# The first feed-forward's beginning: one written order for three engines, constant matmuls where the matrix engine waits, the norm weight loaded as rows, 1/rms by a square root

## Chip, cores and metric

The kernel runs on one core of a Trainium2 chip. The metric is the device time of one execution in microseconds (us); several executions are made and the median is given. The core has five engines with a queue of instructions each: TensorE (PE, matrix products; its weight loads are shown apart as PEld), VectorE (DVE), ScalarE (ACT), GpSimd (POOL) and SyncE (SP), which here only issues DMA transfers. An engine takes its queue strictly in order; an instruction whose operands aren't ready holds up all that stand behind it. PE writes to PSUM, eight banks of 128 x 512 floats; the other data lies in SBUF with 128 partitions.

## What is computed

One encoder layer over two independent sequences of 512 tokens with 1024 channels, in float32: a half-step SwiGLU feed-forward, a mixing block (attention and a matrix memory), a second half-step feed-forward, and a norm. The change touches only the beginning of the first feed-forward:

```python
def rms_norm(x, g):
    y = x * lax.rsqrt(jnp.mean(x * x, axis=-1, keepdims=True) + EPS)
    return y * g

def swiglu(x, w_gate, w_up, w_down):
    return (jax.nn.silu(x @ w_gate) * (x @ w_up)) @ w_down

x = x + 0.5 * swiglu(rms_norm(x, ffn1_norm), ffn1_w_gate, ffn1_w_up, ffn1_w_down)
```

`w_gate` and `w_up` are 1024 x 2816, 22 blocks of 128 columns.

## The kernel before

**Products.** Each float32 matrix is split into a high part, rounded to the format that PE multiplies in one pass (`fp32r`), and a low part, the rest; a product is high x high + high x low + low x high. So each 128 x 512 piece of x and each weight costs ACT one cast (high part) and DVE one subtraction (low part). Gate and up, and the two sequences (`x_prompt`, s = 0, and `x_sample`, s = 1), are combined as the two rows and two columns of a 2 x 2 product with seven multiplications; the seven right-hand operands are the tiles `xc[B11]`, `xc[B21]`, `xc[B22]`, `xc[T1]` to `xc[T4]`. Two of them, B11 and B21, are x_prompt's lower and upper four groups of 128 channels alone; the other five need sums with x_sample.

**The beginning** (from line 1229). x comes in four blocks of 128 tokens per sequence (`load_x`, tile `raw`). `rows_rstd` squares each block, the left half on DVE and the right half on ACT, sums them, and takes 1/rms by a bit trick with three Newton steps, twelve DVE instructions on 128 x 4 elements (`rstd_cols`, `rsqrt_cols`). `turn` transposes a group of 128 channels on PE with the tile `ident` into a PSUM bank, `keep_x` copies it to SBUF on ACT and stores it in `xbuf`. `bcast_psum` turns 1/rms into a 128 x 512 tile with four transposes. `first_x` scales a group (`scaled`: times the norm weight `g1`, times 1/rms; DVE) and splits it (`put`: high on ACT, low on DVE). While x_sample is being prepared, PE begins the products that need x_prompt alone: `up.begin(j, W)` makes for column block j the first product (12 matmuls, B11), parks it in DRAM (`kept`), and makes the second (B21, 12 more). Ten blocks, `AHEAD`, are begun so: 240 matmuls. Then `up.rest` runs the other products (PSUM tiles `pss` and `pst`) of all 22 blocks.

**What sets the order.** A scheduler places the instructions on each engine by priority, as the code is written; `shifted(n)` moves a piece in priority, `tc.keep_in_program_order` (`pin`) keeps an instruction at its written place among the pinned ones of its engine. Weights come by `fetch_w` into tiles `wr` (four buffers) and are split into tiles `w` (four). All loads and stores of this part are issued by SP in the order of its queue. PSUM tiles named `mm` have three banks, `pss` and `pst` two each, `pso` one. Eight matmuls on the tile `ones` (line 1231) stand at the very beginning of PE. `g1` is loaded by POOL, element by element (line 123), and so are the weights of later norms and gates (`mix_gains`, written behind step 13 of `up.rest` but put by POOL's queue at the program's start).

## Time and profile before

| | us |
|---|---|
| median of 3 runs | 2079.39 (2077.46 to 2080.35) |
| the profiled execution, its own time | 2079.39 |
| its span, first to last instruction | 2077.5 |
| PE busy / DVE busy / ACT busy | 2059.7 / 1547.5 / 901.6 |
| PE at the first product of x and a weight | 18.18 |
| first product behind the ten begun blocks (`pss`) | 79.17 |

In the profile a row of the timeline gives the start, the time from the first start to the last end of the instructions that it merges, the engine, the line, the operation, out <- in, the shape and the count; in brackets the idle time before it and who ended it. The time of one instruction contains its fill and drain, which overlap with the next: three in a row take less than three times one. In the table by stretches the columns are the stretch, its length, the busy time of PE, PEld, DVE, ACT and POOL with the number of instructions, then the clock that PE was granted (1 is full), the mean busy share of the DMA engines, and GB/s.

### The profile page before, as it was taken

The page shows a single profiled execution, that of the slowest core. Times are in us where ns is not written, and L with a number is a line of the kernel's source. Part 1 is how long each engine was busy: PE and PEld are TensorE (multiplying, and loading weights), DVE is VectorE, ACT ScalarE, POOL GpSimd, SP SyncE. Part 2 cuts the span into 40 slices and gives each one's busy share as a digit, 9 for nine tenths or more (in the row PEclk, how much of TensorE's full clock was granted, in tenths as well). Part 3 has the DMA queues.
Part 4 walks back from the last instruction along what each step waited for, and adds up shares of the span by engine and source line. Part 5 has one row for each costly group of instructions (what it writes and reads, how often), then busy time and mean ns, then how long its engine had stood idle before and what let it go on. Part 6 is the DMA issues. An engine that isn't in the chain of part 4 may idle for free.

```text
span 2077.5 us, 27122 instructions
## 1 busy us (share of the span) xinstructions
PE 2059.7 (99%) x9451; PEld 1689.1 (81%) x9451; DVE 1547.5 (74%) x2798; ACT 901.6 (43%) x1653; POOL 103.7 (5%) x118
## 2 busy tenths in 40 slices
PE   8999999999999999999999999999999999999998
PEld 6888888888888877888877788888888888888887
DVE  7888888786797897575567645545888888796697
ACT  6544444442234566463344443323544444443224
POOL 1000000001003000100120000002000000000001
PEclk9999999999999999999999999999999999999999
DMA  9656555699766654777675245677656555599753
GB/s 280 206 171 195 193 172 183 197 338 365 267 218 239 219 159 170 260 240 271 218 270 176 102 152 183 204 255 239 210 168 220 176 190 182 166 346 350 267 204 125
DMA packets 307064, 454.31 MB, mean 219 GB/s; under 512 B 20064, under 2 KB 178864, under 8 KB 305904
## 3 DMA queue, kind: packets, MB, share of 16 engines
q1 hardware_dynamic: 304912, 446.87, 64.0%
q0 software_dynamic: 1872, 5.46, 0.8%
q8 instruction: 74, 1.21, 0.2%
q14 instruction: 62, 0.51, 0.1%
q10 hardware_dynamic: 144, 0.26, 0.0%
HBM read 285.63 MB, written 166.89 MB: 218 GB/s over the span
## 4 chain that ended last, share of the span: by engine, by line
PE 94%; DVE 2%; DMA 1%; ACT 1%; issue 0%; SPq 0%; ACTq 0%; DVEq 0%
PE mm L770 20%; PE pss L333 17%; PE pst L333 11%; PE mm L333 10%; PE mm L589 8%; PE pst L589 4%; PE pss L589 4%; PE mm L754 4%; PE pso L589 3%; PE pso L1044 1%; PE pss L1017 1%; PE pso L754 1%; PE pst L1036 1%; PE pso L1180 1%; PE pst L770 1%; PE pss L770 1%
## 5 line engine op out<-in xcount | busy, mean ns | idle before, releaser
L770 PE MATMUL mm<-xh,w 128*128 128x512 f32 x896 | 290.4, 394 | 0.0
L333 PE MATMUL pss<-xc,w 128*128 128x512 f32 x1056 | 256.3, 391 | 0.4 <-DVE t L364 0.4
L333 PE MATMUL mm<-xc,w 128*128 128x512 f32 x1056 | 253.1, 390 | 2.0 <-ACT w L291 1.0
L333 PE MATMUL pst<-xc,w 128*128 128x512 f32 x1056 | 253.8, 389 | 0.0
L333 PEld LDWEIGHTS pss<-xc,w 128*128 128x128 f32 x1056 | 196.9, 188 | 47.6 <-DVE t L364 7.0
L333 PEld LDWEIGHTS mm<-xc,w 128*128 128x128 f32 x1056 | 197.4, 188 | 44.8 <-ACT w L291 1.9
L333 PEld LDWEIGHTS pst<-xc,w 128*128 128x128 f32 x1056 | 198.1, 188 | 41.5 <-ACT t L368 0.4
L770 PEld LDWEIGHTS mm<-xh,w 128*128 128x128 f32 x896 | 167.7, 188 | 33.6
L589 PE MATMUL mm<-rt,w 128*128 128x512 f32 x765 | 178.8, 389 | 0.0
L770 PE MATMUL mm<-xl,w 128*128 128x512 f32 x448 | 176.3, 394 | 0.0
L589 PEld LDWEIGHTS mm<-rt,w 128*128 128x128 f32 x765 | 143.5, 188 | 29.8
L291 ACT ACTIVATE w<-t 128x512 fp32r<-128x512 f32 x176 | 106.9, 627 | 139.0 <-issue 55.2
L292 DVE TENSOR_TENSOR w<-t,w 128x512 fp32r<-128x512 f32 x176 | 118.1, 688 | 55.7 <-ACT w L291 53.8
L333 PE MATMUL pss<-xc,f 128*128 128x512 f32 x528 | 126.8, 389 | 0.0
L333 PEld LDWEIGHTS pss<-xc,f 128*128 128x128 f32 x528 | 99.1, 188 | 20.6
L672 ACT ACTIVATE w<-wr 128x512 fp32r<-128x512 f32 x72 | 45.1, 632 | 138.5 <-PE pso L589 65.2
L672 ACT ACTIVATE w<-t 128x512 fp32r<-128x512 f32 x82 | 51.8, 632 | 107.4 <-PE pst L589 62.4
L770 PEld LDWEIGHTS mm<-xl,w 128*128 128x128 f32 x448 | 84.3, 188 | 16.6
L589 PE MATMUL pss<-rt,w 128*128 128x512 f32 x396 | 93.7, 389 | 0.0
L589 PE MATMUL pst<-rt,w 128*128 128x512 f32 x396 | 93.7, 389 | 0.0
L239 ACT ACTIVATE w<-wr 128x1024 fp32r<-128x1024 f32 (+1 forms) x56 | 57.2, 1027 | 74.0 <-PE mm L770 30.3
L589 PEld LDWEIGHTS pst<-rt,w 128*128 128x128 f32 x396 | 74.3, 188 | 15.4
(359 smaller groups left out, 3653.6 us busy)
## 6 DMA issues: line engine op xcount, KB each, us to landing
rt<-rbuf SPq DMA_DIRECT2D x154, 512.0 KB, 5.5
wpark<-w SPq DMA_DIRECT2D x104, 512.0 KB, 3.4
w<-wpark SPq DMA_DIRECT2D x104, 512.0 KB, 4.6
wr<-in_ffn_w_gate_dram SPq DMA_DIRECT2D x62, 512.0 KB, 5.3
rbuf<-tab SPq DMA_DIRECT2D x102, 256.0 KB, 4.0
wr<-in_ffn_w_up_dram SPq DMA_DIRECT2D x44, 512.0 KB, 4.6
rbuf<-f SPq DMA_DIRECT2D x72, 256.0 KB, 4.0
wr<-in_w_in_dram SPq DMA_DIRECT2D x36, 512.0 KB, 6.0
```

The lines of the kernel that those rows point to most:

```text
L239: pin(nc.scalar.activation(hi, raw, AF.Copy))
L291: pin(nc.scalar.activation(t[:, 0], src, AF.Copy))
L292: pin(V_.tensor_tensor(t[:, 1], src, f(t[:, 0]), op=ALU.subtract))
L333: nc.tensor.matmul(p, a[:, k, :], xt[:, b, k, :], start=(first and k == 0 and i == 0), stop=(k == HK_ - 1 and i == 2), skip_group_check=True)
L589: nc.tensor.matmul(p, u[:, a, d * P:(d + 1) * P], r[:, b, ts], start=(first and q == 0 and k == 0), stop=(q == len(us) - 1 and k == 2), sk ...
L672: nc.scalar.activation(hi, src, AF.Copy)
L754: nc.tensor.matmul(p[b][:, :N], a[:, k, bs], w_[:, kl, :], start=(k == 0 and i == 0), stop=(k == KD - 1 and i == 2))
L770: nc.tensor.matmul(p, a[:, k, :], b, start=(k == 0 and i == 0), stop=(k == n - 1 and i == 2))
L1017: nc.tensor.matmul(p, qT[:, h, b * P:(b + 1) * P], kv[:, hk * 2 + j, :], start=(j == 0), stop=(j == 1))
L1036: nc.tensor.transpose(p[:, b * P:(b + 1) * P], Ps[b][:, kb * P:(kb + 1) * P], ident)
L1044: nc.tensor.matmul(po, Vst[:, kv_, hk, :], w, start=(kv_ == 0 and i == 0), stop=(kv_ == 3 and i == 1))
L1180: nc.tensor.matmul(po, vm[:, a, t, hs_], b, start=(t == 0 and n == 0), stop=(t == 3 and n == 2))
```

## The change

1. `g1` is no longer loaded element by element by POOL but as eight rows of 128, issued by ACT, and transposed by one small PE transpose.
2. `mix_gains` gets a tile of step 13 (`h[0]`) and copies from it first, so that POOL's loads can only run then.
3. The eight matmuls on `ones` are replaced by constant matmuls 128 x 512 on a tile `hot` (`busy(n)`): six at the start, two behind each of the first three blocks of x, three behind the last and three behind the broadcast of 1/rms, 18 in all. Their result isn't used.
4. x_prompt is transposed block by block as it arrives, into seven banks at once, instead of group by group.
5. 1/rms is ACT's square root and DVE's reciprocal in place of the twelve DVE steps. The dummy activation at the start now loads the table with the root, and a second one behind the root of x_sample loads the table with Silu.
6. The beginning is written as a list of steps that pins ACT's and DVE's order (`eps`, for the roots, is now set at the program's start): copies, scalings, high and low parts, weights in halves of four channel groups, squares of x_sample, parked products. Blocks 0 and 1 run both of their products in it; the third waits until x_sample's 1/rms is there.
7. SP's order: the first weight in two halves right behind x_prompt; the up-weight of block 0 is fetched later, and the weight of block 3 earlier.

**PE, the program's start.** Before the change (`pst_93` is the bank of the constant matmuls, `raw_267` x_prompt, `rs_352` 1/rms):

```order
L1231 MATMUL pst_93<-ones 128x128 x8
L1251 MATMUL mm_354<-ident,raw_267 128x128 x4
L1251 MATMUL pss_361<-ident,raw_267 128x128 x4
L1251 MATMUL pst_368<-ident,raw_267 128x128 x4
L1251 MATMUL mm_375<-ident,raw_267 128x128 x4
L1251 MATMUL pss_382<-ident,raw_267 128x128 x4
L1251 MATMUL pst_389<-ident,raw_267 128x128 x2
L213 MATMUL pst_413<-ident,rs_352 128x128 x4
```

In the change, PE from the last block of x_prompt to the first products (`mm_94<-xc_316` are the constant matmuls, `raw_260` x_prompt, `cs_38_336` 1/rms, `w_406` and `w_407` the weights of column blocks 0 and 1):

```order
L1253 MATMUL mm_334<-ident,raw_260 128x128
L1235 MATMUL mm_94<-xc_316 128x512 x3
L1321 MATMUL pst_389<-ident,cs_38_336 128x128 x4
L1253 MATMUL pst_394<-ident,raw_260 128x128 x4
L1235 MATMUL mm_94<-xc_316 128x512 x3
L333 MATMUL mm_435<-xc_316,w_406 128x512 x7
L333 MATMUL mm_448<-xc_316,w_407 128x512 x2
L333 MATMUL mm_435<-xc_316,w_406 128x512 x3
L333 MATMUL mm_448<-xc_316,w_407 128x512 x3
```

The broadcast of 1/rms stood behind six groups and now stands behind all blocks of seven groups, which by then are transposed but for the last block; constant matmuls stand on both sides of it.

**ACT, behind x_prompt.** Before, from the last high part of x_prompt (`R_285<-raw_268` with `cs` are squares of x_sample, L341 and L348 the first and second product of a block):

```order
L278 ACTIVATE xc_419<-t_18_281 128x512
L1270 ACTIVATE R_285,cs_55_523<-raw_268 128x512
L1270 ACTIVATE tab_286,cs_56_524<-raw_268 128x512
L1256 ACTIVATE R_285<-pss_568 128x512
L348 ACTIVATE f_19_282<-mm_432 128x512
L672 ACTIVATE f_9_272<-wr_555 128x512
L341 ACTIVATE f_20_283<-mm_494 128x512
```

In the change, from the same place (L1369 parks a first product, L1342 squares x_sample, L1395 is its root, L1377 is `gate`, the second product):

```order
L1346 ACTIVATE xc_317<-t_18_274 128x512
L1369 ACTIVATE f_20_276<-mm_448 128x512
L1342 ACTIVATE xc_318,cs_41_402<-raw_261 128x1024
L1353 ACTIVATE w_408<-wr_313 128x512 x2
L1257 ACTIVATE R_278<-pss_496 128x512
L1257 ACTIVATE tab_279<-pst_501 128x512
L1395 ACTIVATE cs_42_403<-cs_41_402,eps 128x4
L1396 ACT_TABLE_LOAD
L1396 ACTIVATE warm<-ones 128x1
L291 ACTIVATE w_565<-wr_563 128x1024
L291 ACTIVATE w_629<-wr_627 128x1024
L1377 ACTIVATE f_19_275<-mm_435 128x512
```

The second product of block 0, `mm_435`, is now taken out of its bank behind the squares, the root, a table load and the weights 3 and 4; a second square of x_sample that stands between the two casts and the two copies is left out of these rows.

**POOL, the program's start.** Before (`gain`, `gbias` and `hn` are `mix_gains`' tiles):

```order
L123 DMA g_84<-in_ffn_norm_dram 128x8x1
masks.py:197 MEMSET ident 128x128
L229 COPY wr_311<-raw_267 128x1
L691 DMA gain_96<-in_mix_norm_dram 128x8x1
L691 DMA gain_97<-in_ffn_norm_dram 128x8x1
L692 DMA gbias<-in_mlstm_gate_bias_dram 128x16
L693 DMA hn<-in_mlstm_head_norm_dram 128x4x1
```

In the change (`t_15_271` is `h[0]` of step 13):

```order
masks.py:197 MEMSET ident 128x128
L690 COPY gain_97<-t_15_271 128x8
L692 DMA gain_97<-in_mix_norm_dram 128x8x1
L692 DMA gain_98<-in_ffn_norm_dram 128x8x1
L693 DMA gbias<-in_mlstm_gate_bias_dram 128x16
L694 DMA hn<-in_mlstm_head_norm_dram 128x4x1
```

`g1` is gone from POOL's queue, and the other four loads stand behind a copy that waits for step 13. From the transposes of x_sample's last groups on, the order of PE, DVE and ACT is the same in both programs.

```diff
@@ -120,16 +120,16 @@
         return ap.bitcast(F32)
 
     g1 = cpool.tile([P, KD], F32, name="g1")
-    nc.gpsimd.dma_start(g1, I["ffn1_norm"][0].rearrange("(k p) -> p k", p=P))
-
+    eps = cpool.tile([P, 1], F32, name="eps")
+    nc.vector.memset(eps, EPS)
 
     ident = cpool.tile([P, P], F32, name="ident")
     make_identity(nc, ident)
     ones = cpool.tile([P, P], F32, name="ones")
     nc.vector.memset(ones, 1.0)
-    pw = PT()[:, 0:P]
+    pw = MM()
     warm = cpool.tile([P, 1], F32, name="warm")
-    nc.scalar.activation(warm, ones[:, 0:1], AF.Silu)
+    nc.scalar.activation(warm, ones[:, 0:1], AF.Sqrt)
...
                 if i == at:
-                    hook()
+                    hook(h[0])
...
-    def mix_gains():
+    def mix_gains(behind):
         pin = tc.keep_in_program_order
+        pin(nc.gpsimd.tensor_copy(gm, behind[:, 0:KD]))
         for t, n in ((gm, "mix_norm"), (g2, "ffn2_norm")):
             pin(nc.gpsimd.dma_start(t, I[n][0].rearrange("(k p) -> p k", p=P)))
...
-    for _ in range(8):
-        pin(nc.tensor.matmul(pw, ones, ones, start=True, stop=True))
+
+    def busy(n):
+
+        for _ in range(n):
+            pin(nc.tensor.matmul(pw, hot[:, 0:P], hot, start=True, stop=True))
+
...
...
+    def load_x(s, b):
+        nc.sync.dma_start(raws[s][:, b, :], xins[s][b * P:(b + 1) * P, :])
+
+    def turn(s, k, b, p):
+        return nc.tensor.transpose(p[:, b * P:(b + 1) * P], raws[s][:, b, k * P:(k + 1) * P], ident)
+
+    def keep_x(s, k, p, xt, eng=None):
+
+        i = eng.tensor_copy(xt, p) if eng else nc.scalar.activation(xt, p, AF.Copy)
         nc.sync.dma_start(xbuf[s][:, k, :], xt)
+        return i
 
     orow = up.ring.rows["o"]
 
-    def rows_rstd(s, engines):
-
...
+    def squares(s, b, sq, engines, pin=lambda i: i):
+        for i in range(2):
+            x_, to = raws[s][:, b, i * S:(i + 1) * S], sq[i][:, b:b + 1]
+            if engines[i] is V_:
+                pin(V_.scalar_tensor_tensor(orow[3 + i], x_, 1.0, x_, op0=ALU.mult, op1=ALU.mult, accum_out=to))
+            else:
+                pin(nc.scalar.activation(orow[3 + i], x_, AF.Square, accum_out=to))
+
+    def square_cols():
+        return [spool.tile([P, 4], F32, tag="cs4", bufs=4, name=nm("cs4")) for _ in range(2)]
+
+    def rows_rstd(sq, between=None):
+        pin(V_.tensor_tensor(sq[0], sq[0], sq[1], op=ALU.add))
+        pin(nc.scalar.activation(sq[1], sq[0], AF.Sqrt, scale=1.0 / D, bias=eps))
+        if between:
+            between()
+        pin(V_.reciprocal(sq[1], sq[1]))
+        return sq[1]
 
     def scaled(to, x_, k, R_):
-        V_.scalar_tensor_tensor(to, x_, g1[:, k:k + 1], R_, op0=ALU.mult, op1=ALU.mult)
-
-    load_x(0)
-    raw0 = up.fetch(0, (0,), raws[0][:, 1, 0:1])
-    load_x(1)
-    raw1 = [up.fetch(j, (0,))[0] for j in (1, 2)]
+        return V_.scalar_tensor_tensor(to, x_, g1[:, k:k + 1], R_, op0=ALU.mult, op1=ALU.mult)
+
     x0 = up.ring.rows["x"]
     x0r = orow[:2] + up.ring.rows["s"] + orow[5:7] + orow[2:3]
...
+    for b in range(4):
+        load_x(0, b)
+    raw0 = [wpool.tile([P, KD, P], F32, tag="wr", bufs=4, name=nm("wr"))]
+    for a in range(2):
+        nc.sync.dma_start(half(raw0[0], a), half(up.v[0], a)[:, :, 0:P])
+    load_x(1, 0)
+    raw1 = up.fetch(1, (0,))
+    for b in range(1, 4):
+        load_x(1, b)
+    raw1 += up.fetch(2, (0,))
+    g1row = orow[6][0:KD, 0:P]
+    pin(nc.scalar.dma_start(g1row, I["ffn1_norm"][0].rearrange("(k p) -> k p", p=P)))
+    raws0 = raw0 + raw1
+    for i in (B11, B21, T2_):
+        xc[i] = xc_tile()
+    hot = xc[B11][:, 0, 0, :]
+    nc.vector.memset(f(hot), 1.0)
+    busy(6)
+    banks = [PT(), PT()]
+    pin(nc.tensor.transpose(banks[1][:, 0:KD], g1row, ident[0:KD, 0:KD]))
+    pin(V_.tensor_copy(g1, banks[1][:, 0:KD]))
+    banks += [b() for b in (PS, PS, PO, MM, MM)]
+    sq = square_cols()
+    for b in range(4):
+        for k, p in enumerate(banks):
+            pin(turn(0, k, b, p))
+        squares(0, b, sq, (V_, nc.scalar), pin)
+        if b < 3:
+            busy(2)
+    pin(keep_x(0, 0, banks[0], x0r[0]))
+    rs = rows_rstd(sq, lambda: pin(keep_x(0, 1, banks[1], x0r[1], V_)))
+    busy(3)
+    R0 = PT()
+    for b in range(4):
+        pin(nc.tensor.transpose(R0[:, b * P:(b + 1) * P], rs[:, b:b + 1].to_broadcast([P, P]), ident))
+    banks.append(PT())
+    for b in range(4):
+        pin(turn(0, KD - 1, b, banks[-1]))
+    busy(3)
+
+    def keep(k, eng=None):
+        pin(keep_x(0, k, banks[k], x0r[k], eng))
+
+    def lo(k):
+        t = xc[B11 if k < HK_ else B21]
+        pin(V_.tensor_tensor(t[:, 1, k % HK_, :], x0[k], f(t[:, 0, k % HK_, :]), op=ALU.subtract))
+
+    sq = square_cols()
+
+    def square1(b, eng=None):
+        x_, to = raws[1][:, b, :], sq[0][:, b:b + 1]
+        junk = xc[T2_].rearrange("p a k c -> p (a k c)")
+        if eng:
+            pin(V_.scalar_tensor_tensor(junk[:, 2 * S:4 * S], x_, 1.0, x_, op0=ALU.mult, op1=ALU.mult, accum_out=to))
+        else:
+            pin(nc.scalar.activation(junk[:, 0:2 * S], x_, AF.Square, accum_out=to))
+
+    W = [w8_tile() for _ in range(2)]
+    def hi(k):
+        pin(nc.scalar.activation(xc[B11 if k < HK_ else B21][:, 0, k % HK_, :], x0[k], AF.Copy))
+
+    def sc(k):
+        pin(scaled(x0[k], x0r[k], k, R0))
+
+    def wh(j, a):
+        w = wt[j][:, :, a]
+        pin(nc.scalar.activation(w[:, 0], half(raws0[j], a), AF.Copy))
+
+    def wl(j, a):
+        w = wt[j][:, :, a]
+        pin(V_.tensor_tensor(w[:, 1], half(raws0[j], a), f(w[:, 0]), op=ALU.subtract))
+
+    wt = [w8_tile() for _ in range(3)]
+    W = [{B11: part(w, 0), B21: part(w, 1)} for w in wt]
+    X = [None] * 3
+
+    def first(j):
+        X[j] = MM()
+        product(X[j], W[j][B11], xc[B11], True)
+
+    def park(j):
+        up.kept[j], t = kept[j], up.ring("k")
+        pin(nc.scalar.activation(t, X[j], AF.Copy))
+        nc.sync.dma_start(kept[j][0], t)
+
+    def second(j):
+        product(X[j], W[j][B21], xc[B21], False)
+
+    def gate(j):
+        t = up.ring("k")
+        pin(nc.scalar.activation(t, X[j], AF.Silu))
+        nc.sync.dma_start(kept[j][1], t)
+
+    p1 = {}
+
+    def turn1(k):
+        for kk, bank in ((k, PS), (k + HK_, PT)):
+            p1[kk] = bank()
+            for b in range(4):
+                (turn if k else lambda *a: pin(turn(*a)))(1, kk, b, p1[kk])
+
+    def keep1(k):
+        for kk, kr in ((k, orow[3]), (k + HK_, orow[4])):
+            (keep_x if k else lambda *a: pin(keep_x(*a)))(1, kk, p1[kk], kr)
+
+    with shifted(-400):
+        for step in (wh, 0, 0), (keep, 2), (keep, 3), (sc, 0), (hi, 0), (wl, 0, 0), (keep, 4), (sc, 1), (hi, 1), (lo, 0),                 (wh, 1, 0), (sc, 2), (hi, 2), (lo, 1), (keep, 5), (sc, 3), (hi, 3), (lo, 2), (wl, 1, 0), (square1, 0),                 (wh, 0, 1), (lo, 3), (first, 0), (first, 1), (sc, 4), (hi, 4), (wl, 0, 1), (keep, 6), (sc, 5), (lo, 4),                 (hi, 5), (park, 0), (keep, 7), (sc, 6), (lo, 5), (hi, 6), (wh, 1, 1), (sc, 7), (lo, 6), (hi, 7), (wl, 1, 1), (lo, 7),                 (park, 1), (second, 0), (turn1, 0), (second, 1), (square1, 1), (wh, 2, 0), (wh, 2, 1), (wl, 2, 0), (wl, 2, 1), (square1, 2),                 (keep1, 0), (square1, 3, V_):
+            step[0](*step[1:])
+        pin(nc.scalar.activation(sq[1], sq[0], AF.Sqrt, scale=1.0 / D, bias=eps))
+        pin(nc.scalar.activation(warm, ones[:, 0:1], AF.Silu))
+        pin(V_.reciprocal(sq[1], sq[1]))
+    gate(0)
+    gate(1)
     up.begin(2, W[2])
-    rs = rows_rstd(1, (nc.scalar, nc.scalar))
-    raw0 += up.fetch(0, (1,))
     R1 = orow[2]
-    V_.tensor_copy(R1, bcast_psum(rs))
-    for i in (T2_, T1, T3, B22, T4):
+    with shifted(-100):
+        V_.tensor_copy(R1, bcast_psum(sq[1]))
+    for i in (T1, T3, B22, T4):
         xc[i] = xc_tile()
     x1 = up.ring.rows["s"] + [orow[5]]
     for k in range(HK_):
         x1l, x1u = x1[2 * k % 4], x1[(2 * k + 1) % 4]
-        for t, kk, bank, kr in ((x1l, k, PS, orow[3]), (x1u, k + HK_, PT, orow[4])):
-            p = turn(1, kk, bank)
-            keep_x(1, kk, p, kr)
-            scaled(t, p, kk, R1)
+        if k:
+            turn1(k)
+            keep1(k)
+        scaled(x1l, p1[k], k, R1)
+        scaled(x1u, p1[k + HK_], k + HK_, R1)
         for j in ((3,), (4, 5), (6, 7), (8, 9))[k]:
-            up.begin(j, up.left(j))
+            with shifted(-100):
+                w = up.left(j)
+            up.begin(j, w)
+        if k == 2:
+            raw0 = up.fetch(ORDER[0])
         put(xc[B22], k, x1u)
         right_sums(xc, k, x0[k], x0[k + HK_], x1l, x1u)
     up.begun()
```

40 lines of the change are left out of this document (removed).

## The prediction

> **What bounds the kernel now.** I read the page first: the share of busy time, then the chain of waits.
>
> ```profile
> span 2077.5 us, 27122 instructions
> PE 2059.7 (99%) x9451; PEld 1689.1 (81%) x9451; DVE 1547.5 (74%) x2798; ACT 901.6 (43%) x1653; POOL 103.7 (5%) x118
> PE 94%; DVE 2%; DMA 1%; ACT 1%; issue 0%; SPq 0%; ACTq 0%; DVEq 0%
> ```
>
> TensorE (PE) is busy 99% of the span and carries 94% of the chain: whatever else the change does, it can gain only the 17.8 us in which PE idles, or PE work that it takes away. It takes none of the products away. Next the table by stretches of time, to see where those 17.8 us lie.
>
> ```profile
> 4.60:8.00 3.40, 0.52 (x3) 0.14 (x1) 1.13 (x4) 1.18 (x4) 2.27 (x4) 0.97 0.95 227
> 11.40:14.80 3.40, 3.31 (x17) 2.91 (x16) 1.56 (x10) 2.88 (x8) 0.24 (x1) 0.52 1.16 244
> 14.80:18.20 3.40, 2.28 (x20) 1.80 (x18) 3.00 (x4) 3.40 (x7) 0.00 (x0) 1.00 1.03 380
> 100.00:400.00 300.00, 300.00 (x1316) 246.20 (x1316) 250.79 (x390) 130.97 (x218) 0.00 (x0) 1.00 0.56 182
> ```
>
> From 100 us on PE does not stop; the change must earn its gain in the first 80 us. The rows also show the granted clock (third number from the end): behind a stretch with PE busy 0.52 of 3.40 us stands one at half clock, and behind a full one the full clock. Last the timeline of PE, then VectorE (DVE) and ScalarE (ACT), over that beginning.
>
> ```profile
> 18.18 0.50 PE L333 MATMUL mm<-xc,w 128*128 128x512 f32 x1 [0.54 <-ACT xc L278]
> 22.71 11.21 PE L333 MATMUL mm<-xc,w 128*128 128x512 f32 x48 [0.27 <-DVE w L292]
> 33.76 0.60 PE L213 MATMUL pst<-ident,rs 128*128 128x128 f32 x4
> 36.48 4.86 PE L333 MATMUL mm<-xc,w 128*128 128x512 f32 x20 [0.77 <-ACT w L291]
> 65.47 13.86 PE L333 MATMUL mm<-xc,w 128*128 128x512 f32 x60
> 79.17 2.88 PE L333 MATMUL pss<-xc,w 128*128 128x512 f32 x12
> 85.18 3.04 PE L333 MATMUL pss<-xc,w 128*128 128x512 f32 x12 [0.41 <-DVE t L364]
> ```
>
> The first product starts at 18.18 and PE runs without a gap only from 22.71; one more wait, 0.77 us, is for the fourth weight. 240 matmuls (ten blocks of columns, 24 each) stand before the `pss` products at 79.17. One costs 0.228 us (60 in 13.7); a group of four transposes 0.44 us (0.60 less the overlap), 0.11 each. From the transposes at 65 us to 79.17, and on to the wait at 85.18, the order of every engine is the same in both programs, so 79.17 is my finishing post: what PE gains up to there is the gain of the whole.
>
> **The chain ahead of the first product.**
>
> ```profile
> 4.33 0.69 DVE L1268 SCALAR_TENSOR_TENSOR R<-raw 128x512 f32<-128x512 f32 x1 [3.32 <-DMA raw<-in_x_prompt_dram]
> 5.77 0.69 DVE L1268 SCALAR_TENSOR_TENSOR R<-raw 128x512 f32<-128x512 f32 x1 [0.74 <-DMA raw<-in_x_prompt_dram]
> 8.49 0.69 DVE L1268 SCALAR_TENSOR_TENSOR R<-raw 128x512 f32<-128x512 f32 x1 [2.02 <-DMA raw<-in_x_prompt_dram]
> 9.92 0.69 DVE L1268 SCALAR_TENSOR_TENSOR R<-raw 128x512 f32<-128x512 f32 x1 [0.73 <-DMA raw<-in_x_prompt_dram]
> g<-in_ffn_norm_dram POOLq DMA_DIRECT2D x1, 4.0 KB, 7.4
> 5.85 0.93 POOL L691 DMA_DIRECT2D gain<-in_mix_norm_dram  x1
> ```
>
> The four blocks of x arrive 1.44, 2.72 and 1.43 us apart. The long gap is where the gain `g1` is under way: 4 KB, element by element, issued by POOL, 7.4 us to land. The change loads it as eight rows and moves POOL's four other small loads (the first issued at 5.85) out of the beginning, so I let the third gap fall to the others: 9.92 - 1.28 = 8.64. In the rest of the stretch the DMA moved 380 GB/s (14.80:18.20), at which 512 KB takes 1.38 us: 4.33 + 3 x 1.38 = 8.5. I take 8.3, allowing that the second gap had a share of the same disturbance; the bounds are 8.3 and 9.92. The eight rows of `g1` are now ahead of the transposes in PE's order. A load like it isn't in the trace: at best it is there with x, at worst it takes 7.4 us again and is there at about 9.5, inside the bound 9.92. Nearest is the first block of x, in use at 4.33; the rows are issued one table load later (1.28, a row below), so 5.6, and PE then makes up two blocks (14 transposes and 4 fillers, 2.5 us) by 8.1. I take nothing for it.
>
> ```profile
> 9.91 0.63 ACT L1270 ACTIVATE tab<-raw 128x512 f32<-128x512 f32 x1 [0.71 <-DMA raw<-in_x_prompt_dram]
> 10.54 0.58 ACT L1256 ACTIVATE f<-mm 128x512 f32<-128x512 f32 x1
> 10.72 0.16 DVE L1271 TENSOR_TENSOR cs<-cs,cs 128x4 f32<-128x4 f32 x1
> 13.11 0.16 DVE L192 SCALAR_TENSOR_TENSOR rs<-rs,rs 128x4 f32<-128x4 f32 x1
> 15.20 1.41 DVE L1275 SCALAR_TENSOR_TENSOR t<-f,g,pst 128x512 f32<-128x512 f32 x2 [1.93 <-ACT t L1256]
> 25.75 2.09 DVE L279 TENSOR_TENSOR xc<-t,xc 128x512 fp32r<-128x512 f32 x3
> 2054.91 0.30 ACT L1433 ACTIVATE fs<-cs,eps 128x4 f32<-128x4 f32 x1 [5.39 <-DVE cs L205]
> ```
>
> Before, 5.28 us pass from the last block (9.92) to the first scaled row (15.20): squares and their sum until 10.88, twelve small DVE steps until 13.27, then PE is still in transposes at half clock. After: sum at +0.96; ACT, having copied one bank, takes the root (0.30, the row at 2054.91 is the same operation) until +1.4; DVE copies a bank meanwhile (0.6) and takes the reciprocal (0.17) until +1.75; four transposes 0.60; first scaled row at +2.5, so at 10.8, 4.4 us earlier. The fillers (18 of 0.23 us) lie in PE's waits: three before the broadcast end at 8.3 + 7 x 0.11 + 0.7 = 9.8, ahead of the reciprocal at 10.05. Without that cover they would cost 0.7.
>
> Then DVE sets the pace in the written order: 8 scalings at 0.66 (two in 1.41), 8 low parts and 4 half weights at 0.60, together 12.5 us, and some 0.1 of waits for ACT's high parts: the last low part ends at 23.4. Before, the last ended at 27.84 (25.75 + 2.09). PE follows and has nearly all of the 48 matmuls of two blocks done by then.
>
> **What stands behind it, the price of the written order.** ACT's queue now has, in this order: the last high part, a parked product, a square of x_sample, two half weights, a square, two copies, the root, a table load, the cast of weights 3 and 4, and only then `gate(0)`, which frees the PSUM bank of the third PE block.
>
> ```profile
> 17.45 1.71 ACT L278 ACTIVATE xc<-t 128x512 fp32r<-128x512 f32 x3
> 15.07 1.07 ACT L291 ACTIVATE w<-wr 128x1024 fp32r<-128x1024 f32 x1
> 673.36 1.28 ACT L890 ACT_TABLE_LOAD   x1
> 674.65 0.23 ACT L890 ACTIVATE fa<-fa 128x32 f32<-128x32 f32 x1
> 30.01 5.34 DMA wr<-in_ffn_w_gate_dram
> 76.76 1.29 DVE L292 TENSOR_TENSOR w<-t,w 128x512 fp32r<-128x512 f32 x2
> ```
>
> Casts cost 0.53 each (three in 1.71). The last scaling ends at 23.4 - 1.9 = 21.5; high part, parked product and square (its width isn't in the trace: between one 1024-wide cast, 1.07, and two 512-wide squares, 1.26; I take 1.07) bring ACT to 23.7, the half weight to 24.3. DVE: two low parts (1.29) and the last square (1.2 to 1.4, two of 0.69 at most; 1.3) until 26.9. Root 27.2, table load 28.5, dummy 28.7, two casts of 0.96 to 30.6, `gate(0)` 31.2. PE meanwhile: reciprocal at 27.4, broadcast 0.6, 11 matmuls 2.5, six transposes 0.65, so 31.2 as well. From 31.3 PE is dense, with 60 matmuls and 14 of 32 x_sample transposes done. Left are 180 x 0.228 + 18 x 0.11 = 43.0 us, which ends at 74.3. The same count checks on before: behind 36.48 stood 176 matmuls and 20 transposes, 42.3 us, and it took 42.7. With 0.25 us for the joints between engines: 74.55, 4.6 us before 79.17.
>
> The weights come in time: before, the fourth was issued at 30.01 and awaited for 5.34, since a buffer had gone to the other weight of block 0. Now that one is fetched later, the fourth has its buffer from the start and stands in SP's queue right after five stores of x, and ACT wants it only at 28.7. If it came as late as before (35.4) all of the gain from this place on would go, 4.1 us; the range does not reach to that, since the wait before was for a buffer. **Sum:** -4.6 us. The profiled execution took 2079.39 us, 1.9 above its span and equal to the median of the three runs: **2074.8 us**.
>
> **Rivals.**
>
> *The clock stays at half during the loads* (2076.2). For it: stretches with little PE work were followed by half clock. Then after the last block 7 transposes at 0.21 and 3 fillers at 0.45 end at 11.1 instead of 9.8, later than the reciprocal by 1.05, the broadcast 0.8 instead of 0.6, and joints: 1.4 lost. Against: with fillers PE is busy some 1.2 of each 1.38 us. [...]
>
> *ACT is later than its list* (2076.2): the first parked product overwrites a row of x whose store must have landed.
>
> ```profile
> 15.13 3.67 SPq L1257 DMA_DIRECT2D xbuf<-f  x2
> xbuf<-f SPq DMA_DIRECT2D x2, 256.0 KB, 6.1
> ```
>
> Before, that store landed at 15.13 + 6.1 = 21.2; ACT now wants the row at about 19.8. If the store is no sooner, ACT stands for 1.4 and `gate(0)` comes as much later. Against: x and the weights, which stand ahead of the store in SP's queue, come sooner without POOL's loads. A table switch that costs 1.4 more than its 1.28 would do the same; but at 673.36 the next ACTIVATE began 1.29 later. [...]
>
> *x comes no sooner* (2076.4): if the long gap isn't `g1`'s doing, 1.6 of the 4.6 are lost.
>
> *Slower than before: the small loads in their new place.* They now run behind step 13 of the first feed-forward, near 310 us, where PE is back to back.
>
> ```profile
> 312.41 0.41 SPq L232 DMA_DIRECT2D wr<-in_ffn_w_up_dram  x1
> 321.40 0.69 DVE L314 TENSOR_TENSOR t<-wr 128x512 f32<-128x512 f32 x1
> wr<-in_ffn_w_up_dram SPq DMA_DIRECT2D x1, 512.0 KB, 4.9
> 14.56 0.24 POOL L694 TENSOR_SCALAR hn<-hn 128x4 f32<-128x4 f32 x1 [5.60 <-DMA hn<-in_mlstm_head_norm_dram]
> ```
>
> Before, they held the DMA from 5.85 to 14.5. A weight load has 9.0 - 4.9 = 4.1 us to spare here; it decides when it is held up by 4.1 + 4.6 us or more, which is the whole 8.7 of those loads. With no slack left PE loses 8.7: 2083.5. Against: beside `g1` the x blocks lost 1.3 us, not 7.4.
>
> **Numbers.** Forecast 0.74 (own range 2073.8 to 2075.7, by the joints, the squares and 8.3 against 8.64), clock 0.07, ACT late 0.06, x no sooner 0.05, slower 0.08. A measurement of this kernel tells about 0.2% from no change, 4.2 us: below 2075.2 is faster. Three quarters of the forecast's case lie there, 0.57; the rest of it and the three small losses are no change, 0.35; slower 0.08. Range 2073.5 to 2077.6: it takes in the small losses with a second of them in part, and leaves out the slow case.
>
> **What would show it.** Right: the square of x's last block near 8.3, first scaled row near 10.8, last low part near 23.4, `gate(0)` near 31, `pss` near 74.5, clock 1.00 throughout, no PE wait from 31.5 on but that of 0.4 before the third `pss` group, and unchanged rows after 100 us. Wrong: a clock of 0.5 between 5 and 15 us, a third gap of 2.7 us, ACT waiting for a store, a PE wait near 310 us, or a wait that takes the place of the 0.77 for weight 3.

## The result, and the profile after

The change took 2074.26 us (median of 13 runs, 2073.53 to 2075.51), the kernel before 2079.57 us (13 runs, 2077.29 to 2081.20). The ratio is 0.9976 with an interval of 0.9968 to 0.9985: faster by 0.24%. The same kernel was run twice more beside the experiments, with ratios of 0.9972 (0.9962 to 0.9983) and 0.9973 (0.9964 to 0.9983). The forecast was 2074.8 us. The profiled execution took 2074.45 us, 1.75 us above its span.

The page of the changed kernel, its first rows and the chain's shares by engine:

```profile
span 2072.7 us, 27121 instructions
PE 2059.4 (99%) x9454; PEld 1689.0 (81%) x9454; DVE 1544.9 (75%) x2783; ACT 903.3 (44%) x1649; POOL 101.7 (5%) x117
PE 97%; DVE 1%; DMA 1%; ACT 1%; issue 0%; ACTq 0%
```

PE's busy time is the same as before (2059.7 us), although the constant matmuls now take 6.95 us instead of 3.64: the transposes of x, some of which ran at a granted clock of 0.50 to 0.52 before (8.00 to 14.80), take 8.89 us instead of 11.22, and the rest is spread over small differences. The span is 4.8 us shorter, so the idle time of PE fell from 17.8 to 13.3 us, and its share of the chain rose from 94% to 97%.

The table by stretches of time, for the same slices as before (each engine's busy time and instructions, the granted clock, the DMA engines' share, GB/s):

```profile
4.60:8.00 3.40, 3.40 (x25) 2.94 (x26) 2.17 (x7) 1.94 (x6) 0.00 (x0) 1.00 1.01 394
11.40:14.80 3.40, 2.04 (x8) 0.81 (x6) 3.40 (x7) 2.79 (x6) 0.00 (x0) 1.00 1.09 372
14.80:18.20 3.40, 3.40 (x9) 2.65 (x10) 3.40 (x6) 2.98 (x6) 0.00 (x0) 0.53 1.09 349
100.00:400.00 300.00, 300.00 (x1316) 246.24 (x1315) 252.44 (x393) 131.03 (x218) 4.17 (x6) 1.00 0.55 180
```

The first slice moves 394 GB/s where it moved 227, and PE works in it for 3.40 us where it worked 0.52. From 11.40 to 18.20, and on to 23.44, DVE has no idle time left. Its timeline shows where the gain came from and where part of it went again:

```profile
4.88 0.68 DVE L1267 SCALAR_TENSOR_TENSOR R<-raw 128x512 f32<-128x512 f32 x1
8.47 0.69 DVE L1267 SCALAR_TENSOR_TENSOR R<-raw 128x512 f32<-128x512 f32 x1 [0.64 <-DMA raw<-in_x_prompt_dram]
10.87 0.75 DVE L1283 SCALAR_TENSOR_TENSOR t<-f,g,pst 128x512 f32<-128x512 f32 x1 [0.74 <-PE pst L1321]
22.76 0.68 DVE L1332 TENSOR_TENSOR xc<-t,xc 128x512 fp32r<-128x512 f32 x1
30.32 0.69 DVE L1403 COPY R<-pst 128x512 f32<-128x512 f32 x1 [2.71 <-DMA xbuf<-R]
32.37 2.35 DVE L292 TENSOR_TENSOR w<-wr,w 128x1024 fp32r<-128x1024 f32 x2
```

The last square starts at 8.47 (before: 9.92), the first scaled row at 10.87 (15.20), and the last low part ends at 23.44 (27.84). The row at 30.32 is the copy of `R1`, the broadcast 1/rms of x_sample; it stands 2.71 us, and a store ends its wait. Before, the same copy started at 34.39 and waited for PE's broadcast alone:

```profile
34.39 0.69 DVE L1307 COPY R<-pst 128x512 f32<-128x512 f32 x1 [0.89 <-PE pst L213]
```

In the change `R1` lies as before in `orow[2]`, and group 7 of x_prompt was parked in that same row and is still on its way to `xbuf`. Of the 2.71 us about 0.74 would go to PE's broadcast in any case (the first variant below). The low parts of weights 3 and 4 stand behind it on DVE, and PE waits for them:

```profile
33.64 2.56 PE L333 MATMUL mm<-xc,w 128*128 128x512 f32 x10 [1.56 <-DVE w L292]
76.14 2.88 PE L333 MATMUL pss<-xc,w 128*128 128x512 f32 x12
81.58 2.88 PE L333 MATMUL pss<-xc,w 128*128 128x512 f32 x12
```

The first `pss` product, the finishing post of the prediction, comes at 76.14 instead of 79.17: 3.03 us sooner. The third has lost the 0.41 us wait that it had before and comes at 81.58 instead of 85.18, 3.60 sooner. The rest of the 4.8 us, 1.2, lies further on; below it is seen to differ as much between executions of one program.

SP's timeline tells why the store is late, ACT's the rest of what the prediction listed behind the last low part:

```profile
19.49 3.21 SPq L1258 DMA_DIRECT2D xbuf<-tab  x1
23.27 0.40 SPq L1258 DMA_DIRECT2D xbuf<-R  x1
```

```profile
20.20 0.59 ACT L1257 ACTIVATE R<-pst 128x512 f32<-128x512 f32 x1
27.42 1.28 ACT L1396 ACT_TABLE_LOAD   x1
28.71 0.20 ACT L1396 ACTIVATE warm<-ones 128x1 f32<-128x1 f32 x1
28.82 1.99 ACT L291 ACTIVATE w<-wr 128x1024 fp32r<-128x1024 f32 x2
30.72 1.06 ACT L1377 ACTIVATE f<-mm 128x512 f32<-128x512 f32 x2
```

Row `R` is written at 20.20, its store is issued only at 23.27, since the store of group 6 ahead of it takes 3.21 us to issue and that of a parked product follows; it lands some 7.0 us later, just ahead of 30.32. The DMA engines are full all that time (a share of 1.10 from 23.27 to 30.30).

### The profile page after: what moved, and what is told of

It is laid out like the page before. It is cut to its first block, busy times and chain, and to the rows that moved or that the text cites. A ratio compares the mean times of both kernels' runs of the same rounds, so it can differ in the third digit from the quotient of the medians.

```text
span 2072.7 us, 27121 instructions
## 1 busy us (share of the span) xinstructions
PE 2059.4 (99%) x9454; PEld 1689.0 (81%) x9454; DVE 1544.9 (75%) x2783; ACT 903.3 (44%) x1649; POOL 101.7 (5%) x117
## 4 chain that ended last, share of the span: by engine, by line
PE 97%; DVE 1%; DMA 1%; ACT 1%; issue 0%; ACTq 0%
PE mm L771 21%; PE pss L333 18%; PE pst L333 12%; PE mm L333 11%; PE mm L589 8%; PE pst L589 4%; PE pss L589 4%; PE mm L755 4%; PE pso L589 3%; PE pss L1018 1%; PE pso L1045 1%; PE pso L755 1%; PE pst L1037 1%; PE pso L1181 1%; PE pst L771 1%; PE pss L771 1%
## 5 line engine op out<-in xcount | busy, mean ns | idle before, releaser
L589 PEld LDWEIGHTS pss<-rt,w 128*128 128x128 f32 x396 | 74.3, 188 | 15.4
```

Of the source, the lines that this page charges most:

```text
L589: nc.tensor.matmul(p, u[:, a, d * P:(d + 1) * P], r[:, b, ts], start=(first and q == 0 and k == 0), stop=(q == len(us) - 1 and k == 2), sk ...
```

## The experiments

Theory A: the gain is what comes sooner at the head (x, 1/rms, the written order), less the wait of the `R1` copy for group 7's store. Rivals: the gain is the clock's, held up by the constant matmuls (B); the store's wait costs nothing in the end (C). The table gathers what the traces and the runs showed; ratios are to the kernel before, run in the same series, whose medians were 2079.57, 2079.89, 2080.06 and 2079.35 us.

| kernel | first scaled row | copy of R1 (its wait for a store) | first pss | median, us | ratio (interval) |
|---|---|---|---|---|---|
| before | 15.20 | 34.39 (none) | 79.17 | | |
| the change | 10.87 | 30.32 (2.71) | 76.14 | 2074.26 | 0.9976 (0.9968 to 0.9985) |
| the change, 2nd | 11.29 | 29.81 (1.95) | 75.68 | 2075.17 | 0.9972 (0.9962 to 0.9983) |
| the change, 3rd | 10.81 | 30.60 (3.06) | 76.44 | 2074.25 | 0.9973 (0.9964 to 0.9983) |
| R1 in group 6's row | 11.85 | 29.16 (none) | 75.73 | 2075.08 | 0.9978 (0.9969 to 0.9988) |
| R1 in group 6's row, stores in order | 11.49 | 29.19 (none) | 75.26 | 2075.05 | 0.9976 (0.9966 to 0.9986) |
| R1 in group 6's row, two stores by POOL | 12.09 | 29.38 (none) | 75.73 | 2074.29 | 0.9977 (0.9966 to 0.9987) |
| small steps for 1/rms | 13.29 | 30.60 (none) | 76.58 | 2076.36 | 0.9981 (0.9972 to 0.9990) |
| no fillers | 10.78 | 34.08 (none) | 79.97 | 2078.29 | 0.9992 (0.9983 to 1.0002) |
| no fillers, stores in order | 11.91 | 30.82 (2.34) | 76.66 | 2075.39 | 0.9976 (0.9967 to 0.9985) |
| g1 by POOL | 11.91 | 30.61 (2.08) | 76.56 | 2075.56 | 0.9982 (0.9973 to 0.9990) |
| four gains early | 13.41 | 31.84 (1.71) | 77.70 | 2077.05 | 0.9988 (0.9979 to 0.9996) |
| both loads as before | 13.27 | 32.88 (1.90) | 78.76 | 2076.96 | 0.9987 (0.9977 to 0.9997) |
| before, with the loads alone | 12.76 | 32.74 (none) | 78.08 | 2079.07 | 0.9996 (0.9986 to 1.0005) |

**R1 in another row.** The row of group 6 is stored earlier.

```diff
-    R1 = orow[2]
+    R1 = orow[6]
```

> The change with one edit: the broadcast 1/rms of x_sample goes to the row of x group 6 instead of that of group 7. Theory: the 1.56 us PE wait at 33.64 us comes from DVE's copy of that broadcast, which stood from 27.6 to 30.32 for the store of group 7's row. The store of group 6 is issued some 0.6 to 3 us sooner, so the copy starts near 28.1, the low part of weight 3 ends near 31.3 instead of 33.5, the PE wait falls under 0.3 us, the first pss product begins near 74.6 instead of 76.14, and the time falls by about 1.5 us to 2072.8. Rival: the wait is ACT's late cast of weight 3 behind the table load; then DVE's low part stays near 33 and the time stays at 2074.3.

The trace of this variant, DVE and PE:

```profile
29.16 0.69 DVE L1403 COPY tab<-pst 128x512 f32<-128x512 f32 x1 [0.74 <-PE pst L213]
31.21 2.35 DVE L292 TENSOR_TENSOR w<-wr,w 128x1024 fp32r<-128x1024 f32 x2
32.15 3.03 PE L333 MATMUL mm<-xc,w 128*128 128x512 f32 x12
75.73 2.88 PE L333 MATMUL pss<-xc,w 128*128 128x512 f32 x12
```

The copy waits for PE's broadcast alone, the low parts of weights 3 and 4 start at 31.21 instead of 32.37, PE's wait of 1.56 us is gone, and from the first scaled row to the first `pss` product it takes 63.88 us instead of 65.27. So the copy's wait for the store is what delayed PE. The head came 1 us later in this execution (PE's second pair of transposes took 0.63 us instead of 0.38; the last section has more). In the time the expected 1.5 us do not show: the median is 2075.08, not to be told from the change, and whether the other executions had as late a head isn't known.

**The change again, twice.**

> The changed kernel once more, beside the edits of the same call. Median within 0.1% of the first series (2074.26 us): 2073.5 to 2075.5. Should the saving after 85 us (some 1.2 us of small PE waits between 700 and 1450 us) be the change's doing, those waits are missing again and the span is again 4.5 to 5 us shorter than before's 2077.5 although the first pss product comes only 3 us earlier. If it is scatter between executions, the waits differ from those of the first profile and the span follows the first pss product within 1 us.

> The changed kernel a third time, for comparison in this call: median 2074 to 2075.3 us, first pss product 75.6 to 76.2, the wait of the R1 copy for the store of group 7 at 1.9 to 2.8 us.

The rows of the copy and of the first `pss` product, of the second and then of the third profile of the change:

```profile
29.81 0.69 DVE L1403 COPY R<-pst 128x512 f32<-128x512 f32 x1 [1.95 <-DMA xbuf<-R]
75.68 2.88 PE L333 MATMUL pss<-xc,w 128*128 128x512 f32 x12
```

```profile
30.60 0.69 DVE L1403 COPY R<-pst 128x512 f32<-128x512 f32 x1 [3.06 <-DMA xbuf<-R]
76.44 2.88 PE L333 MATMUL pss<-xc,w 128*128 128x512 f32 x12
```

The third execution had the earliest head (10.81) and the latest product, the second the reverse. (The third one's copy and product lie outside what was expected of it.) What decides is the copy: from it to the product it is 45.82, 45.87 and 45.84 us in the three. In the other four kernels of the table where the copy waits for the store it is 45.84 to 45.95. So in the traces, wherever that wait stands, the store's landing sets the end of this stage, not the head. Behind the third `pss` product the three spans run 1991.1, 1992.2 and 1990.6 us, before 1992.3, and in the variant with the loads alone 1993.0: a program differs from itself there by 1.6 us, so what seems to be gained after 85 us (1.2, 0.1 and 1.7 us of the 4.8, 4.2 and 5.0 us by which the three spans, 2072.7, 2073.3 and 2072.5, are shorter than before's) isn't shown to be the change's. Nor is it shown to be chance: the three medians lie 5.3, 4.9 and 5.1 us below before's, and of before there is one trace only.

**1/rms by twelve small steps again.**

```diff
-        pin(nc.scalar.activation(sq[1], sq[0], AF.Sqrt, scale=1.0 / D, bias=eps))
         if between:
             between()
-        pin(V_.reciprocal(sq[1], sq[1]))
-        return sq[1]
+        return rstd_cols(sq[0], 4, D)
```

> The change, with 1/rms of x_prompt worked out in twelve small VectorE steps again, as in the kernel before (there 2.4 us from the sum of squares to the last step), where the change needs a root, a reciprocal and the joints between ACT and DVE (some 0.75 us). If the root was worth its 1.6 us on the chain ahead of the first scaled row: last square 8.5, first scaled row 12.4 to 12.6 (change: 10.87), first pss product 77.6 to 77.9 (76.14), median 1.6 us above the change, so 2075.9. Rival, the wait of the R1 copy for the store of group 7 (2.71 us in the change) takes up a delay at the head: first scaled row as above, but that wait shorter by 1.6 and the pss product near 76.2, no difference in time.

The trace of this variant: first scaled row and copy of `R1` on DVE, the row of group 7 on ACT, its store on SP.

```profile
13.29 0.75 DVE L1281 SCALAR_TENSOR_TENSOR t<-f,g,pst 128x512 f32<-128x512 f32 x1 [0.89 <-PE pst L1319]
30.60 0.69 DVE L1401 COPY R<-pst 128x512 f32<-128x512 f32 x1 [0.74 <-PE pst L213]
22.59 0.59 ACT L1257 ACTIVATE R<-pst 128x512 f32<-128x512 f32 x1
23.21 0.39 SPq L1258 DMA_DIRECT2D xbuf<-R  x1
```

The root is worth more at the head than was expected: the first scaled row is 2.4 us later than in the change. But row `R` is written 2.4 us later and its store is issued at 23.21, as in the change (23.27): SP's queue had that much slack, the copy no longer waits for it, and the first `pss` product is only 0.1 to 0.9 us later than in the change's three profiles. In this one trace most of the delay is taken up, as the rival had it. The times say otherwise in part: the median is 1.2 us above that of the change in the same series, and all eleven runs lie above that median (2075.29 or more against 2075.17). How much of the delay is left in an average execution, between 0 and the 1.6 us of the other theory, one trace doesn't tell.

**No constant matmuls behind the first six.** The twelve in PE's waits are left out (the `busy` calls between the blocks of x and around the broadcast).

```diff
-        if b < 3:
-            busy(2)
...
-    busy(3)
```

> The change without the twelve constant matmuls behind the blocks of x and around the broadcast; the six at the start stay. Theory of the forecast: PE is idle between the blocks, the clock is half from 8 us to 12 or 15 us, the broadcast ends 1 to 1.4 us later (first scaled row near 12.1 instead of 10.87) and so does all behind, pss near 77.3, time 2075.5. Rival: transposes alone keep the clock up, or the half clock hides behind DVE, which sets the pace; first scaled row within 0.3 us of 10.87 and the time within 0.3 us.

SP's and ACT's timelines of this variant:

```profile
10.80 3.54 SPq L1258 DMA_DIRECT2D xbuf<-t  x3
23.34 0.60 ACT L1365 ACTIVATE f<-mm 128x512 f32<-128x512 f32 x1 [3.64 <-DMA xbuf<-f]
```

It lost 3.8 us at the `pss` product, but through something else than it was made for: without the fillers the scheduler put the store of group 0 behind three others on SP, and the first parked product waited 3.64 us for the row that it overwrites. This is the prediction's rival "ACT is later than its list", with more than twice its price. It says nothing on the clock, so it was made again with the stores held in the order of the rows:

```diff
+        i2 = nc.sync.dma_start(xbuf[s][:, k, :], xt)
+        if s == 0:
+            pin(i2)
```

> The change without the constant matmuls behind the first six, and with the stores of x_prompt to xbuf issued in the order in which the rows are made, so that SP doesn't put off the store of group 0 as it did in the variant without fillers. If the stores' order was what that variant lost (a parked product waited 3.64 us for a store): that wait is under 0.5 us, the first pss product comes at 75.5 to 76.5 and the median is within 0.5 us of the change, though the granted clock is again under 1.00 in one or more of the slices from 8 to 25 us. If the clock is what the fillers buy: the wait for the store is gone as well, but the low clock stretches PE's work, PE waits or runs late, first pss product at 77.5 or later and a median 1.4 us or more above the change.

The table by stretches of this second variant:

```profile
8.00:11.40 3.40, 2.15 (x16) 1.68 (x17) 2.25 (x7) 2.62 (x8) 0.00 (x0) 1.00 1.10 354
11.40:14.80 3.40, 1.63 (x10) 1.08 (x10) 2.89 (x5) 2.95 (x7) 0.00 (x0) 1.00 1.10 371
14.80:18.20 3.40, 3.38 (x9) 2.16 (x9) 3.40 (x7) 3.15 (x7) 0.00 (x0) 0.54 1.08 351
```

The clock falls to 0.54, as it did in the change's first profile, the `pss` product comes at 76.66, and the time is the change's. The twelve fillers are worth nothing that these runs can show, so rival B falls as far as they go. It is not tested in full: the six constant matmuls at the start and the transposes block by block stand in every variant of the change, and the clock was 1.00 from 8.00 to 14.80 here without fillers, where the kernel before had 0.50 and 0.52. How much of the earlier head is that clock's isn't shown. While the clock is low DVE has no idle time (3.40 of 3.40 us). The head is 1 us later than in the change, for another reason: the third block of x came late, with none of the small loads beside it.

```profile
8.19 0.69 DVE L1269 SCALAR_TENSOR_TENSOR R<-raw 128x512 f32<-128x512 f32 x1 [1.73 <-DMA raw<-in_x_prompt_dram]
```

**The loads, one by one.** First both as before (`g1` by POOL, element by element, and the four small loads at the beginning), then the kernel before with both as in the change, and then each alone.

```diff
+    nc.gpsimd.dma_start(g1, I["ffn1_norm"][0].rearrange("(k p) -> p k", p=P))
-    pin(nc.scalar.dma_start(g1row, I["ffn1_norm"][0].rearrange("(k p) -> k p", p=P)))
...
-                    hook(h[0])
+                    hook()
```

> The change with its loads undone: the norm weight element by element by POOL at the start, and POOL's four other small loads at the start too. Theory: the third gap between the blocks of x is 2.7 us again, the last square starts at 9.9 instead of 8.47, everything behind is 1.4 us later, and the stores wait longer for the DMA, so the first pss product begins at 77.5 to 79 instead of 76.14; time 2075.7 to 2077. Rival: the long gap was not these loads' doing; the gaps stay at 1.35 us and the time at 2074.3.

> The kernel before with only the loads changed: the norm weight as eight rows issued by ACT, POOL's four other loads behind step 13. Theory: last square of x_prompt at 8.5 instead of 9.92, first scaled row near 13.8 instead of 15.20, first pss product near 77.8 instead of 79.17, time about 2078.2 (1.4 less). Rival: the chain behind the last block (transposes at half clock, twelve small DVE steps) or the late fourth weight takes it back; pss stays within 0.4 us of 79.17.

> The change with g1 alone loaded as before (element by element, by POOL, 4 KB); the four other small loads stay late. If g1 makes the long third gap, as the prediction has it: gaps between the squares as in the variant with both undone (2.2 and 2.6 us for the second and third), last square at 9.9 to 10.9 instead of 8.5 to 8.9, and the first pss product 1.3 to 2.6 us later than the change's (75.7 to 76.1), median 1 to 2 us above it. If the four other loads make it: gaps of 1.4, last square 8.5 to 8.9, no difference in time.

> The change with g1 as rows, but with POOL's four other small loads at the beginning again. If g1 makes the third gap: gaps of 1.4 us, last square 8.5 to 8.9, first pss product within 0.5 us of the change's, no difference in time. If the four other loads make it: third gap 2.5 us or more, last square 9.6 to 10.9, first pss product 1 to 2.5 us later.

The four squares on DVE with `g1` alone by POOL:

```profile
4.42 0.69 DVE L1268 SCALAR_TENSOR_TENSOR R<-raw 128x512 f32<-128x512 f32 x1 [2.85 <-DMA raw<-in_x_prompt_dram]
5.86 0.69 DVE L1268 SCALAR_TENSOR_TENSOR R<-raw 128x512 f32<-128x512 f32 x1 [0.74 <-DMA raw<-in_x_prompt_dram]
8.05 0.69 DVE L1268 SCALAR_TENSOR_TENSOR R<-raw 128x512 f32<-128x512 f32 x1 [1.50 <-DMA raw<-in_x_prompt_dram]
9.52 0.69 DVE L1268 SCALAR_TENSOR_TENSOR R<-raw 128x512 f32<-128x512 f32 x1 [0.77 <-DMA raw<-in_x_prompt_dram]
```

The last two squares, and POOL's first load, with the four others early:

```profile
7.41 0.69 DVE L1266 SCALAR_TENSOR_TENSOR R<-raw 128x512 f32<-128x512 f32 x1 [0.92 <-DMA raw<-in_x_prompt_dram]
11.01 0.69 DVE L1266 SCALAR_TENSOR_TENSOR R<-raw 128x512 f32<-128x512 f32 x1 [2.90 <-DMA raw<-in_x_prompt_dram]
1.44 1.10 POOL L691 DMA_DIRECT2D gain<-in_mix_norm_dram  x1 [0.15 <-issue]
```

With `g1` alone the gap ahead of the third block is 2.19 us (before: 2.72) and the last square comes 0.6 to 1.1 us later than in the change's profiles, sooner than expected; the `pss` product is 0.1 to 0.9 us later, the median 1.3 us above the change's in the same series. The four others alone do worse, a gap of 3.60 and a last square at 11.01; but without `g1` ahead of them POOL issues them at 1.44 instead of 5.85, right among the blocks of x. With both as before they too come sooner than before (2.88), and the last square only at 10.87. In all four traces with small loads at the start the last square comes at 9.52 or later, in nine of the ten without at 8.38 to 8.89. The tenth is that of the variant without fillers and with the stores in order: a gap of 2.43 us ahead of its third block and a last square at 9.51, without any such load. So the loads slow x, the four others most clearly; the share of `g1` alone, to which the prediction put the long gap down, isn't told from scatter by one trace. In time both loads as before cost about 0.0013 of the whole (0.9987 against 0.9972 to 0.9976), so 2 to 3 us, and the four alone as much.

In the kernel before, the same loads bring little:

```profile
12.76 1.41 DVE L1275 SCALAR_TENSOR_TENSOR t<-f,g,pst 128x512 f32<-128x512 f32 x2 [0.89 <-ACT t L1256]
34.85 5.06 PE L332 MATMUL mm<-xc,w 128*128 128x512 f32 x21 [1.03 <-ACT w L290]
```

The first scaled row is 2.44 us earlier, the wait for weight 3 grows to 1.03 us, and the `pss` product gains 1.09. At the `pss` product the loads alone are worth 1.09 us and the order with the small loads at the start 0.41, against 2.7 to 3.5 together. The sum falls short, but not shown is that the two need each other: with the new order the four loads also ran 3 us sooner than before, so the 0.41 is too low for the order alone.

**Towards a better version.** The row of group 6 with the stores in order; then, without that order, the row of group 6 with the first two stores issued by POOL and the first parked product two places earlier on ACT. The second one's edit, but for the row:

```diff
-        nc.sync.dma_start(xbuf[s][:, k, :], xt)
+        q = nc.gpsimd if s == 0 and k < 2 else nc.sync
+        q.dma_start(xbuf[s][:, k, :], xt)
...
-(wl, 0, 1), (keep, 6), (sc, 5), (lo, 4), (hi, 5), (park, 0), (keep, 7)
+(wl, 0, 1), (park, 0), (keep, 6), (sc, 5), (lo, 4), (hi, 5), (keep, 7)
```

> The change with R1 in the row of group 6 instead of group 7 (no store under way there when R1 is made) and the stores of x_prompt in the order in which the rows are made. If the wait of the R1 copy costs what the variant with the other row alone showed (1.4 us from the first scaled row to the first pss product): R1 copy without a store wait, no PE wait of 1.5 us near 33 us, first scaled row 10.9, first pss product at 74.6 to 74.9, median 1.2 to 1.5 us below the change in the same call. Rival, the gain is lost again in the waits further on (for weights, stores and the third pss group): first pss product at 74.6 to 74.9, but the third pss group waits by as much more, and the median is within 0.4 us of the change.

> The change with R1 in the row of group 6, the stores of the first two rows of x_prompt issued by POOL instead of SP (there they stand behind 2 MB of loads and take 3.4 us to issue), and the first parked product two places earlier in ACT's order. If rows still being stored are what holds PE up after the change: no ACT or DVE wait for a store before 35 us, the PE waits of 0.6 to 1.0 near 20.5 us (for the parked product) and of 0.8 to 1.6 near 33 us gone, first pss product at 74.5 to 74.9 (the 74.55 that the prediction had for the change, corrected by the head's own time), median 0.8 to 1.5 us below the change in the same call. Rival, the DMA engines are full until 35 us (share of 1.05 to 1.13 in every slice), so what is stored sooner makes something else later: a new wait for weight 3 or 4 or for a square of x_sample, first pss product no sooner than 75.3, median within 0.4 us of the change.

The last variant, PE and DVE:

```profile
5.37 0.63 PE L1253 MATMUL pss<-ident,raw 128*128 128x128 f32 x2
10.20 0.38 PE L1253 MATMUL pss<-ident,raw 128*128 128x128 f32 x2
12.09 0.75 DVE L1284 SCALAR_TENSOR_TENSOR t<-f,g,pst 128x512 f32<-128x512 f32 x1 [0.80 <-PE pst L1322]
75.73 2.88 PE L333 MATMUL pss<-xc,w 128*128 128x512 f32 x12
```

No engine waits for a store before 35 us any more, and PE's waits near 20 and 33 us are gone. From the first scaled row to the `pss` product it takes 63.64 us (the other row alone 63.88, with stores in order 63.77; the change 64.39 to 65.63). But in this execution PE was slow for longer: the two transposes at 5.37 hold PE for 0.42 us, those at 10.20 for 0.22, at a granted clock of 1.00 from 4.60 to 11.40; PE is still at them when x has come, and the head is 1.3 us behind the change's third profile. The medians are those of the change in the same series (2074.29 and 2074.25; with the stores in order 2075.05 and 2075.17), and the expected 0.8 to 1.5 us are missing in both. So the traces speak against rival C, since without the wait the stage behind the head is 0.5 to 2 us shorter, while the times speak for it. Whether the three late heads are chance or belong to these variants, and use the gain up, is open. None of them can be called faster than the change.

## Why the prediction was right, and where it was not

- **What bounds, and where the gain lies**: right. What moved for certain lies in the first 85 us; from 100 to 400 us PE is busy for 300.00 us, as before.
- **x comes sooner**: right in size (last square 8.47, forecast 8.3; bounds 8.3 to 9.92). That it is all `g1`'s doing isn't shown: with `g1` alone as before the last square came at 9.52, in a variant without any small load at 9.51, and the four other loads alone made it 11.01. The eight rows of `g1` cost nothing behind the first square, as assumed: they are copied at 4.80, so DVE's first square starts at 4.88 instead of some 4.4, and the second follows nearly at once (0.15 us of wait for x).
- **The root, the fillers, the first scaled row**: forecast 10.8, measured 10.87, 11.29 and 10.81. Without fillers it was 10.78 in one trace, so their cover wasn't needed.
- **DVE paces until 23.4**: 23.44. **Root, table load, casts, `gate(0)`**: the root was to end at 27.2, the load at 28.5, the casts at 30.6, the first `gate(0)` at 31.2; by the rows they end at 27.41, 28.70, 30.81 and about 31.3 (two in a row from 30.72 to 31.78). The load began 0.01 us after the root's end and the next ACTIVATE 1.29 us after the load's start, so the switch held ACT for 1.30 us in all.
- **The step that failed** is "From 31.3 PE is dense" and with it the sum of 43.0 us up to 74.55. The list of what stands behind the written order had ACT's queue in full, but of DVE's only the low parts, the square and the reciprocal; the copy of `R1` behind them was not in it, nor that its row is the one whose store is issued last. Before, it never waited for that store: it came at 34.39, all came later there. In the change it stands 1.95 to 3.06 us on DVE (0.74 of it for PE's broadcast in any case) and costs PE 0.81 to 1.67, and the term of 4.6 us became 3.03, 3.49 and 2.73 in the three profiles. Without that wait the rest of the sum held: 63.64 to 63.88 us from first scaled row to `pss` in the three variants with another row, where the forecast has 74.55 - 10.8 = 63.75. Their heads were 0.7 to 1.3 us later than the forecast's, so no trace has the early head and the free copy together.
- **The rival "ACT is later than its list"** named this very mechanism, a row overwritten while it is being stored, but at the parked product. There it did not come about in the change; it came one row further on, and at the parked product as soon as the stores' order was disturbed (3.64 us).
- **The third `pss` group's wait stays**: wrong by 0.57 us, in the change's favour. It was 6.01 us from the first to the third group before, 5.44 after.
- **The clock is 1.00 throughout**: wrong in one of the three profiles of the change (0.53 from 14.80 to 18.20), and without a price that shows: the third profile, at 1.00 there, reaches `pss` 0.3 us later.
- **The slow rival, the small loads near 310 us**: fell. From 300 to 330 us PE was busy for 30.00 us; the loads, issued from 318.7 on, landed in 2.6 to 3.0 us instead of 6.3 to 7.3.

So the closeness of the time is luck in part, since errors offset each other: the forecast counted 1.1 to 1.9 us too much gain up to the first `pss` product and 0.57 too little at the third, and 0.1 to 1.7 us further on has no cause that these runs show.

## What to carry to other kernels

When a start is made shorter, list for every engine what each of its rows overwrites, and ask whether the earlier content has been stored: a wait that never showed because everything came later is the first to take the gain. Where the end of a stage keeps a constant distance to one instruction over many variants (45.8 us here), that instruction is on the path, and in a trace delays ahead of it cost only what its own wait does not take up; look at the times as well, which here kept more of the delay than the trace did. Leave an instruction out of a scheduled program only with the order of the queues held, or the order is what you measure.

## What the runs showed of the hardware

- How long PE is slow at the start differs between executions of the same rows. Two transposes in a row take 0.66 to 0.69 us instead of 0.38 until some 5.2 us in the change's three profiles, and 0.61 to 0.81 until about 6.6 to 7.7 us in five variants with the same beginning, while the granted clock reads 1.00 from 4.60 to 8.00 in all of them; the durations tell it, the column does not. What makes PE slow there isn't shown.
- Behind 11.40 to 14.80 with PE busy for 2.04 us the clock was 0.53 in one execution of the change (the rows by stretches of time under the result) and 1.00 in another, its third profile, by the same view:

```profile
11.40:14.80 3.40, 2.04 (x8) 0.81 (x6) 3.40 (x7) 2.85 (x6) 0.00 (x0) 1.00 1.09 376
14.80:18.20 3.40, 3.40 (x15) 2.61 (x16) 3.40 (x6) 2.99 (x6) 0.00 (x0) 1.00 1.09 348
```

  Without fillers, 8.00 to 11.40 held transposes alone, for 2.15 us, and the clock stayed at 1.00 into the next slice (11.40 to 14.80).
- A load of 4 KB by single elements landed in 6.8 to 7.4 us among the blocks of x (the kernel before) and in 2.9 to 3.0 us near 320 us (the change). With four small loads among them (2 to 8 KB each) the gap ahead of the fourth 512 KB block was 3.60 us, where the traces without small loads have 1.3 to 1.4; with `g1` alone the gap ahead of the third was 2.19, but 2.43 once without any.
